# Four late sums in the change-over to the down projection, put at other places of a written order

## The chip, the cores and the metric

The kernel runs on one core of one Trainium2 chip. The metric is the device time of one execution, in microseconds (us), as the median of the runs shown. The core has five engines that work side by side, each through its own list of instructions in order: TensorE (PE in the profile, its weight loads PEld) for matrix products, VectorE (DVE) and ScalarE (ACT) for work on elements, GpSimd (POOL) and SyncE (SP). SP and POOL also issue the DMA transfers here. Engines wait for one another, and for transfers, by semaphores.

## The reference

The kernel computes one layer of a hybrid decoder in float32, for 512 tokens of width 2048. Cut to what matters here, the second half of the layer:

```python
up = h @ w_ffn_in                      # [512, 2048] x [2048, 2 * 5632]
a, b = up[..., :D_FF], up[..., D_FF:]
a = causal_conv3(a) + conv_b
f = (gelu(a) * b) @ w_ffn_out          # [512, 5632] x [5632, 2048]: the down projection
y = x + rmsnorm(f, ffn_post_norm)
```

Ahead of it stand the token mixer (linear attention and differential attention on one input projection, then an output projection) and the norms.

## The kernel before, in words

**Products.** A float32 operand is split into a rounded high half and a remainder. ACT writes the high half (line 138 for weights, line 151 for activations), DVE the remainder (lines 139 and 152), and PE takes three products of halves: lines 1298 to 1300 in the up projection, lines 1400 to 1402 in the down projection. A piece of weights of 128 by 1024 numbers, 512 KB, is called a granule. In the down projection a granule feeds 12 products of 128 by 512.

**Seven products for eight.** Both projections of the channel mixer are cut into 2 by 2 blocks, and seven products with sums of blocks take the place of eight (a Strassen scheme in Winograd's form). A unit of work has seven segments, x0, z0, y0, z1, x1, y1 and y2, of two granules each. The sums of weight blocks are made by DVE and by transfers that add in place, which POOL issues. The sums of the token side, s5, s2, s7 and s3, are made from the output of the up projection's units by `token_sums`: s5 = a21 - a22, s2 = s5 - a11, s7 = a11 - a21, s3 = s2 + a12. Each is one DVE instruction of 128 by 512 elements (line 1373), and a store of 256 KB to DRAM (the tensors `sd0` to `sd4`) follows it, issued by SP in `put`. The four tiles come from a pool of two buffers (`tag="sum", bufs=2`). The last group of units hands its four sums over as functions in the list `late_sums`, in the order s5, s2, s7, s3, to be called later. What they store is read again by the last units of the down projection only.

**The order of the work.** Most of the kernel is ordered by a planner that simulates the engines and places each instruction where it expects it to be ready. The change-over from the last up unit `u` to the first two down units `d0` and `d1` is written out by hand in `change_over` and issued by `run_in_order`, which keeps the written order on PE, ACT, DVE and POOL. It walks through 22 granules: the segments x0 of d0; y1, x1, y2 of u; z0, y0, z1, x1 of d0; x0 of d1; y1 and y2 of d0. At each step it first splits the weights up to three granules ahead (`make`), then issues the granule's products, then, behind a segment's second granule, the reading out of the PSUM banks (`out`, through `into`: ACT at line 1406 for the first write of a place, DVE at line 1408 where it adds), and last the functions that `at` has hung on this segment and granule. Instructions that come after the written block (the rest of d1 first) may still be drawn by the planner into places among the block's last ones.

**A bank that is read and continued.** The segments x0, y0, y1 and y2 of a unit add into one pair of banks. So the first product of y2 into a bank waits until y1's reading of that bank is done.

Of the kernel before, what the change touches and what calls it, by code (L numbers as in the profile page):

```python
# [35 lines left out]
def hybrid_layer(ctx: ExitStack, tc: tile.TileContext, x, attn_pre_norm, w_in, w_alpha_up, b_alpha,  # L36
# [1416 lines left out]
    def at(u, seg, g, *fs):  # L1453
        hooks.setdefault((u, seg, g), []).extend(fs)

    def load_unit(u):
        u.t = [load_t(u.block(0, 0, g), u.a) for g in range(2)]
        u.b22, u.b21 = [], []

    def load_b(u, name, i, j, by=None):  # L1460
        getattr(u, name).extend(load(u.block(i, j, g), u.a, by) for g in range(2))

    def add_t(u, name, g):
        tt(u.t[g], u.t[g], getattr(u, name)[g], ALU.add)
# [13 lines left out]
    def prepare_at(c, n, load_at, split_at):  # L1478
        f, g = prepare_parts(c, n)
        at(*load_at, f)  # L1480
        at(*split_at, g)
# [41 lines left out]
    def change_over(u):  # L1523
        d0, d1 = downs[:2]
        order = [(d0, "x0"), (u, "y1"), (u, "x1"), (u, "y2")]
        order += [(d0, g) for g in ("z0", "y0", "z1", "x1")] + [(d1, "x0"), (d0, "y1"), (d0, "y2")]
        at(d0, "x0", 0, lambda: load_b(d0, "b22", 1, 1))
        at(d0, "x0", 0, late_tiles)
        at(d0, "x0", 1, lambda: (add_t(u, "b21", 0), add_t(u, "b21", 1)))
        at(u, "x1", 1, lambda: load_b(d0, "b21", 1, 0))  # L1530
        at(d0, "z0", 1, lambda: load_unit(d1))
        prepare_at(0, "s2", (d0, "x0", 1), (u, "y2", 0))
        prepare_at(0, "s3", (u, "y1", 1), (d0, "z0", 0))
        prepare_at(0, "a12", (u, "x1", 0), (d0, "z0", 1))
        prepare_at(0, "s7", (u, "x1", 1), (d0, "y0", 1))
        prepare_at(0, "a22", (u, "y2", 0), (d0, "z1", 1))
        for g in range(2):
            at(u, "y2", g, lambda g=g: add_t(d0, "b22", g))
        at(d0, "z1", 0, lambda: add_t(d0, "b21", 0))
        at(d0, "x1", 0, lambda: add_t(d0, "b21", 1))  # L1540
        for where in ((d0, "y0", 0), (d0, "x1", 1), (d1, "x0", 0), (d1, "x0", 1)):
            at(*where, lambda: late_sums.pop(0)())
        return order

    order = change_over(ups[-1])
    u = ups[-1]
    u.b21 = [load(u.block(1, 0, g), u.a) for g in range(2)]
# [217 lines left out]
```

## Time and profile before

| | us |
|---|---|
| median of the runs | 2078.0 |
| runs | 2084.13, 2075.84, 2078.0 |
| the profiled execution, its own time | 2077.34 |
| its span, from first to last instruction | 2075.6 |
| PE busy in the span | 2048.7 |
| DVE busy | 1508.4 |
| ACT busy | 1000.0 |
| POOL busy | 291.9 |

A row of the profile's timeline gives the start in us from the beginning of the span, the duration, the engine, the line of the kernel, the operation and `out<-in`; brackets tell how long the engine had stood idle before and what ended the wait. In the table of waits a row reads: who waited, for whom, the sum in us, how many times, the longest. The chain of waits follows the work that ended last back in time. Rows by stretch of time give, for each engine, the busy us and the number of instructions, and then the granted clock of PE (1.00 is full speed), the share of time in which the transfer engines were busy, and GB/s. A row of a transfer ends in the KB of one and the median us from issue to landing.

### The profile page before, as it was taken

The page shows a single profiled execution, that of the slowest core. Times are in us where ns is not written, and L with a number is a line of the kernel's source. Part 1 is how long each engine was busy: PE and PEld are TensorE (multiplying, and loading weights), DVE is VectorE, ACT ScalarE, POOL GpSimd, SP SyncE. Part 2 cuts the span into 40 slices and gives each one's busy share as a digit, 9 for nine tenths or more (in the row PEclk, how much of TensorE's full clock was granted, in tenths as well). Part 3 has the DMA queues.
Part 4 walks back from the last instruction along what each step waited for, and adds up shares of the span by engine and source line. Part 5 has one row for each costly group of instructions (what it writes and reads, how often), then busy time and mean ns, then how long its engine had stood idle before and what let it go on. Part 6 is the DMA issues. An engine that isn't in the chain of part 4 may idle for free.

```text
span 2075.6 us, 35519 instructions
## 1 busy us (share of the span) xinstructions
PE 2048.7 (99%) x14429; PEld 1896.9 (91%) x14429; DVE 1508.4 (73%) x1793; ACT 1000.0 (48%) x1303; POOL 291.9 (14%) x306
## 2 busy tenths in 40 slices
PE   7999999999999999999999999999999999999998
PEld 6799999999988889899999999999999978888886
DVE  5967777666762255977777777777777888988977
ACT  5544444455552243454554554454455654544433
POOL 0112222222200000011011011111110111111100
PEclk9999999999999999999999999999999999999999
DMA  5488888888883354457667578577667886776663
GB/s 213 121 187 185 192 197 182 196 174 200 193 259 125 94 177 146 124 112 197 149 148 195 142 163 191 131 171 179 141 162 196 214 237 185 188 196 182 165 181 122
DMA packets 281465, 358.61 MB, mean 173 GB/s; under 512 B 14848, under 2 KB 223156, under 8 KB 279380
## 3 DMA queue, kind: packets, MB, share of 16 engines
q1 hardware_dynamic: 192148, 259.85, 37.4%
q0 software_dynamic: 84800, 94.38, 30.1%
q10 hardware_dynamic: 4352, 2.10, 0.4%
q8 instruction: 113, 1.85, 0.4%
q14 instruction: 52, 0.43, 0.1%
HBM read 311.72 MB, written 44.56 MB: 172 GB/s over the span
## 4 chain that ended last, share of the span: by engine, by line
PE 93%; DVE 2%; DMA 2%; issue 1%; ACT 1%; POOL 1%; DVEq 0%; SPq 0%; POOLq 0%; ACTq 0%
PE bank L1298 12%; PE bank L1299 12%; PE bank L1300 12%; PE bank L1400 6%; PE bank L1401 6%; PE bank L1402 6%; PE bank L193 3%; PE bank L192 3%; PE bank L194 3%; PE bank L793 3%; PE bank L795 3%; PE bank L794 3%; PE bank L797 2%; PE bank L798 2%; PE bank L799 2%; PE bank L176 2%
## 5 line engine op out<-in xcount | busy, mean ns | idle before, releaser
L138 ACT ACTIVATE ring<-raw 128x1024 fp32r<-128x1024 f32 x315 | 333.7, 1061 | 499.1 <-PE bank L1299 113.1
L139 DVE TENSOR_TENSOR ring<-raw,ring 128x1024 fp32r<-128x1024 f32 x315 | 383.5, 1223 | 259.3 <-ACT ring L138 256.0
L138 ACT ACTIVATE ring<-rt 128x1024 fp32r<-128x1024 f32 x221 | 234.5, 1061 | 259.3 <-PE bank L1299 154.0
L1299 PE MATMUL bank<-al,ring 128*128 128x256 f32 x1280 | 354.0, 277 | 0.0
L1298 PE MATMUL bank<-ah,ring 128*128 128x256 f32 x1280 | 354.0, 277 | 0.0
L1300 PE MATMUL bank<-ah,ring 128*128 128x256 f32 x1280 | 353.9, 277 | 0.0
L139 DVE TENSOR_TENSOR ring<-rt,ring 128x1024 fp32r<-128x1024 f32 x221 | 270.2, 1223 | 91.2 <-ACT ring L138 90.2
L1298 PEld LDWEIGHTS bank<-ah,ring 128*128 128x128 f32 x1280 | 240.5, 188 | 0.1
L1299 PEld LDWEIGHTS bank<-al,ring 128*128 128x128 f32 x1280 | 240.4, 188 | 0.1
L1300 PEld LDWEIGHTS bank<-ah,ring 128*128 128x128 f32 x1280 | 240.4, 188 | 0.0
L1402 PE MATMUL bank<-ring,al 128*128 128x512 f32 x424 | 165.8, 391 | 0.0
L1401 PE MATMUL bank<-ring,ah 128*128 128x512 f32 x424 | 165.7, 391 | 0.0
L1400 PE MATMUL bank<-ring,ah 128*128 128x512 f32 x424 | 153.2, 392 | 2.2 <-DVE acc L1408 2.2
L193 PE MATMUL bank<-ring,ah 128*128 128x512 f32 x280 | 109.8, 393 | 0.0
L192 PE MATMUL bank<-ring,ah 128*128 128x512 f32 x280 | 109.6, 397 | 0.0
L194 PE MATMUL bank<-ring,al 128*128 128x512 f32 x280 | 109.3, 393 | 0.0
L1246 POOL DMA_DIRECT2D raw<-in_w_ffn_in_dram x40 | 51.2, 1309 | 396.4 <-DVE ring L139 396.4
L1400 PEld LDWEIGHTS bank<-ring,ah 128*128 128x128 f32 x424 | 79.9, 188 | 19.7 <-DVE acc L1408 3.1
L1246 POOL DMA_DIRECT2D rt<-in_w_ffn_in_dram x40 | 50.9, 1279 | 325.9 <-DVE ring L139 303.4
L1402 PEld LDWEIGHTS bank<-ring,al 128*128 128x128 f32 x424 | 79.9, 189 | 16.7
L1401 PEld LDWEIGHTS bank<-ring,ah 128*128 128x128 f32 x424 | 79.9, 188 | 16.4
L797 PE MATMUL bank<-ring,ah 128*128 128x256 f32 x320 | 92.1, 288 | 1.0 <-ACT ah L151 1.0
(378 smaller groups left out, 5661.8 us busy)
## 6 DMA issues: line engine op xcount, KB each, us to landing
raw<-in_w_ffn_in_dram SPq DMA_DIRECT2D x96, 512.0 KB, 4.8
raw<-in_w_in_dram SPq DMA_DIRECT2D x56, 512.0 KB, 4.5
raw<-in_w_ffn_out_dram SPq DMA_DIRECT2D x46, 512.0 KB, 6.0
raw<-in_w_in_dram POOLq DMA_DIRECT2D x40, 512.0 KB, 7.2
rt<-in_w_ffn_in_dram SPq DMA_DIRECT2D x40, 512.0 KB, 6.1
rt<-in_w_ffn_in_dram POOLq DMA_DIRECT2D x40, 512.0 KB, 6.2
raw<-in_w_ffn_in_dram POOLq DMA_DIRECT2D x40, 512.0 KB, 6.9
raw<-in_w_o_dram SPq DMA_DIRECT2D x32, 512.0 KB, 3.9
```

The source lines that it names most:

```text
L138: act(hi, raw, AF.Copy)
L139: tt(lo, raw, hi.bitcast(F32), ALU.subtract)
L192: mm(banks[t], ah[:, t, s, :], w[0][:, k, :], start=st, stop=False)
L193: mm(banks[t], ah[:, t, s, :], w[1][:, k, :], start=False, stop=False)
L194: mm(banks[t], al[:, t, s, :], w[0][:, k, :], start=False, stop=sp)
L797: mm(o, sh[:, n, kk, :], wh[:, k, :], start=st, stop=False, **NOW)
L1298: mm(o, wh, sh[:, :, kk, :], start=start and kk == 0 and n == 0, stop=False, **NOW)
L1299: mm(o, wh, sl[:, :, kk, :], start=False, stop=False, **NOW)
L1300: mm(o, wl, sh[:, :, kk, :], start=False, stop=kk == HK - 1, **NOW)
L1400: mm(b[j], sh[:, o:o + P], w[0][:, q, :], start=start and st == 0, stop=False, **NOW)
L1401: mm(b[j], sh[:, o:o + P], w[1][:, q, :], start=False, stop=False, **NOW)
L1402: mm(b[j], sl[:, o:o + P], w[0][:, q, :], start=False, stop=st == 3, **NOW)
```

## The change

One line of `change_over` names the places at which the four functions of `late_sums` are called. A place is a unit, a segment and a granule of it.

```diff
-        for where in ((d0, "y0", 0), (d0, "x1", 1), (d1, "x0", 0), (d1, "x0", 1)):
+        for where in ((d0, "y0", 0), (d0, "y0", 0), (d0, "x1", 1), (d0, "y1", 1)):
             at(*where, lambda: late_sums.pop(0)())
```

In the order of the 22 granules, counted from 0, the calls stood at 10 (s5), 15 (s2), 16 (s7) and 17 (s3). They now stand at 10 (s5), 10 (s2), 15 (s7) and 19 (s3). The functions, their number and their order are as they were:

```python
def add(n, x, y, op):
    def go():
        t = made[n] = fp.tile([P, 2, 256], F32, name=n, tag="sum", bufs=2)
        tt(t, made.get(x, x) if isinstance(x, str) else x, y, op)
        put(n, t)
    return go
```

## The prediction

> **What bounds the kernel now.** I read the busy shares first, then the waits of PE over the whole span, then the chain of waits around the one place that the change touches, and last the timelines of DVE and SP there.
>
> ```profile
> PE 2048.7 (99%) x14429; PEld 1896.9 (91%) x14429; DVE 1508.4 (73%) x1793; ACT 1000.0 (48%) x1303; POOL 291.9 (14%) x306
> ...
> PE bank L159 <- DVE xt L248: 10.6, 2, 9.6
> PE bank L1400 <- DVE acc L1408: 2.2, 1, 2.2
> PE bank L797 <- ACT ah L151: 1.0, 1, 1.0
> ```
>
> PE is busy for all but 27 us of its 2075.6 us. The longest waits are at the start (line 159). The largest after that is a single one of 2.2 us, of a product of the down projection (line 1400) for a reading of a bank by DVE (line 1408). No other exceeds 1.0 us. So a change to this kernel can win only what such waits cost. The chain of waits says what stands behind the 2.2 us:
>
> ```profile
> 1669.75 0.25 DVE s L1373
> 1670.02 7.93 DMA sd4s<-s
> 1678.31 0.34 issue
> 1678.65 0.37 DVE xlo L139
> ...
> 1679.79 0.69 DVE acc L1408
> 1680.52 0.50 PE bank L1400
> ```
>
> A sum of line 1373 is stored at 1670.02, the store takes 7.93 us, and only when it has landed, at 1677.95, does DVE go on; then follow a weight split, the reading of the bank, and PE's product at 1680.52. The DVE timeline shows which sum is which:
>
> ```profile
> 1652.83 0.69 DVE L1373 TENSOR_TENSOR s<-u 128x512 f32<-128x512 f32 x1
> 1654.95 1.23 DVE L152 TENSOR_TENSOR al<-st,ah 128x1024 fp32r<-128x1024 f32 x1 [1.44 <-ACT ah L151]
> ...
> 1667.57 0.69 DVE L1373 TENSOR_TENSOR s<-s,u 128x512 f32<-128x512 f32 x1
> 1668.17 1.22 DVE L139 TENSOR_TENSOR ring<-raw,ring 128x1024 fp32r<-128x1024 f32 x1
> 1669.31 0.68 DVE L1373 TENSOR_TENSOR s<-u 128x512 f32<-128x512 f32 x1
> 1669.91 1.22 DVE L139 TENSOR_TENSOR ring<-rt,ring 128x1024 fp32r<-128x1024 f32 x1
> 1671.05 1.22 DVE L152 TENSOR_TENSOR al<-st,ah 128x1024 fp32r<-128x1024 f32 x1
> 1673.55 1.23 DVE L139 TENSOR_TENSOR ring<-rt,ring 128x1024 fp32r<-128x1024 f32 x1 [1.29 <-ACT ring L138]
> 1678.04 0.69 DVE L1373 TENSOR_TENSOR s<-s,u 128x512 f32<-128x512 f32 x1 [3.27 <-DMA sd4s<-s]
> 1678.65 1.22 DVE L139 TENSOR_TENSOR xlo<-rt,xhi 128x1024 fp32r<-128x1024 f32 x1
> 1679.79 0.68 DVE L1408 TENSOR_TENSOR acc<-acc,bank 128x512 f32<-128x512 f32 x1
> 1680.39 1.22 DVE L1263 TENSOR_TENSOR rt<-rt,raw 128x1024 f32<-128x1024 f32 x1
> 1681.52 0.68 DVE L1408 TENSOR_TENSOR acc<-acc,bank 128x512 f32<-128x512 f32 x1
> ```
>
> The four rows of line 1373 are s5, s2, s7, s3 in this order. s3 at 1678.04 had waited 3.27 us for the store issued at 1670.02, which is that of s7 (added at 1669.31), not that of s2. So s3 writes into s7's buffer: s2 is still an operand of s3 and holds the other one. Behind s3 in DVE's list stand the last split of y2 (1678.65) and the two readings of d0's y1 (1679.79 and 1681.52), one for each bank, and PE's y2 needs these.
>
> **What the stall costs PE.** It is more than 2.2 us:
>
> ```profile
> 1660.00:1675.00 15.00, 15.00 (x68) 12.42 (x67) 13.49 (x15) 7.34 (x8) 2.37 (x2) 1.00 1.05 289
> 1675.00:1690.00 15.00, 12.78 (x49) 9.74 (x48) 10.31 (x11) 5.65 (x7) 1.17 (x1) 0.89 0.82 261
> 1690.00:1705.00 15.00, 15.00 (x68) 12.43 (x67) 12.30 (x12) 10.77 (x13) 2.36 (x2) 1.00 0.66 172
> ...
> 1682.00:1685.40 3.40, 3.38 (x8) 2.48 (x8) 3.40 (x4) 0.18 (x1) 0.63 (x1) 0.50 0.61 226
> ...
> 1700.00:1800.00 100.00, 100.00 (x443) 82.86 (x442) 87.72 (x92) 49.09 (x49) 12.41 (x11) 1.00 0.75 205
> ```
>
> PE started 49 products in the 15 us around the stall, and 68 in the 15 us before and after. At 100 us / 443 = 0.226 us each the 19 missing ones are 4.3 us. The parts: PE's last start before the gap and its next one are
>
> ```profile
> 1677.70 0.61 PE L1400 MATMUL bank<-ring,ah 128*128 128x512 f32 x2
> 1680.52 0.50 PE L1400 MATMUL bank<-ring,ah 128*128 128x512 f32 x1 [2.21 <-DVE acc L1408]
> ```
>
> two products from 1677.70, so the next was due at 1678.15 and came 2.37 us late. Then the granted clock stood at 0.50 from 1682.00 to 1685.40, where 3.4 us do the work of 1.7. The rest, 0.2 us, is the second bank: its reading ended at 1681.52 + 0.68 = 2.2, and its product came at 1682.25, two tenths behind its turn. 2.37 + 1.7 + 0.2 = 4.3 us.
>
> The half clock is counted with the stall because the trace has full clock before and after it, and keeps full clock across shorter gaps: a stretch in which PE idled for 1.9 us, the wait of 1.0 us of line 797 among it, stays at 1.00.
>
> ```profile
> 590.00:600.00 10.00, 8.09 (x70) 7.68 (x69) 9.45 (x13) 6.28 (x11) 0.00 (x0) 1.00 0.45 146
> ```
>
> [...]
>
> **The change, part by part.** Nothing is added or removed: four sums of 0.69 us (each takes 0.60 us of DVE's turn: 1667.57 to 1668.17) and four stores of 256 KB. Each is followed in turn.
>
> *s2, from granule 15 to 10.* It now follows s5, at 1653.43 in before's times. Its operand s5 is DVE's own result just made. DVE was idle there for 1.44 us until 1654.95, for ACT; 0.60 us fit. Cost nothing; if that cover were gone, 0.6 us of DVE, still behind splits made three granules (8 us) ahead. Its store is issued at about 1654.1, where SP had nothing to issue until 1656.21:
>
> ```profile
> 1653.54 0.32 SPq L48 DMA_DIRECT2D sd4s<-s  x1
> 1656.21 0.32 SPq L48 DMA_DIRECT2D st<-sd1a  x1
> ...
> 1668.28 0.34 SPq L48 DMA_DIRECT2D sd4s<-s  x1
> ...
> 1678.76 0.32 SPq L48 DMA_DIRECT2D sd4s<-s  x1
> ```
>
> *s7, from 16 to 15.* It takes the place s2 had, 1667.57, and waits for s5's store. That left at 1653.54 and took 5.2 us (row below), so it has been landed for 8.8 us. Its own store leaves at 1668.28, where s2's did. Cost nothing. DVE has one sum fewer at 1669.31, so the split of y2's first granule comes 0.6 us sooner.
>
> *s3, from 17 to 19.* This is the step that counts. In the list it moves behind the last split of y2 and behind both readings of y1. So that split can go as soon as ACT has the high half:
>
> ```profile
> 1670.95 1.05 ACT L138 ACTIVATE xhi<-rt 128x1024 fp32r<-128x1024 f32 x1
> ```
>
> that is at 1672.0 in place of 1678.65, in the 1.29 us for which DVE now idles ahead of 1673.55. (The split at 1673.55 is that of a granule of d1 which the planner has drawn forward.) y1 ends on PE at 1674.98, by its last product:
>
> ```profile
> 1674.75 0.39 PE L1402 MATMUL bank<-ring,al 128*128 128x512 f32 x1
> ```
>
> Its first bank is complete six products (1.36 us) sooner, so DVE reads it at about 1674.0, or at 1674.7 if d1's split (1673.55 to 1674.7) stays ahead. PE now follows y1 with 14 products drawn forward from d1 (1674.98 to 1678.15, 14 x 0.226 = 3.2 us) before y2. If the planner keeps them, the bank is read 2.8 us in time. If y2 follows y1 directly, PE waits 1674.7 + 0.68 - 1674.98 = 0.4 us at worst, under the 1.0 us that left the clock alone. So the stall goes, with bounds of 3.9 and 4.3 us on the gain; I take 4.3.
>
> What is late next is s3 itself. It comes up on DVE behind the second reading, at about 1675.3 (y1's last product ends at 1675.14) + 0.68 = 1676.0, and waits for s7's store, now issued at 1668.28:
>
> ```profile
> raw<-in_w_ffn_out_dram POOLq DMA_DIRECT2D x1, 512.0 KB, 11.0
> sd4s<-s SPq DMA_DIRECT2D x1, 256.0 KB, 5.2
> ...
> sd4s<-s SPq DMA_DIRECT2D x1, 256.0 KB, 7.9
> ```
>
> With 5.2 us it has landed at 1673.5, with 7.9 us at 1676.2: a wait of 0 to 0.2 us. Behind s3 in DVE's list are the weight sums of line 1263 and the split of d1's second granule of z0, 0.6 + 1.13 + 1.13 = 2.9 us with s3. PE needs that split after y2 (24 products) and z0's first granule (12): 1674.98 + 36 x 0.226 = 1683.1. So s3 may start as late as 1680.2, and the store may take up to 11.9 us. On SP, s3's store stood blocked until 1678.76 with other transfers behind it in the queue, and PE shows no wait for a transfer later; it now goes sooner.
>
> **Sum.** 2077.34 (the profiled execution; 0.66 below the median of 2078.0, inside the runs' 2075.84 to 2084.13) - 4.3 = 2073.0 us. PE is the bound on both sides of the place (no wait of PE in the span is later than this one), so the gain reaches the end.
>
> **The rivals.**
>
> *Part of the stall comes back through the planner (0.09).* The written block fixes only its own order. Behind it the planner places by simulated times, and these change: it drew a granule of d1 ahead of y2 in before, and may place line 1263 or a split ahead of y1's readings. One such piece is 1.13 us; behind 1674.7 it makes PE wait 0.4 + 1.13 = 1.5 us, between the 1.0 that kept the clock and the 2.2 that lost it. The price is 1.5 to 3.2 us: 2074.5 to 2076.2. For it speaks that 1680.39 stands between the two readings; against it, that every later unit has the same join without a wait.
>
> *The clock would have dropped anyway (0.05).* If the half clock belonged to some earlier load and not to the gap, only 2.37 + 0.2 = 2.6 us go: 2074.7. [...] Against it: the clock is full in every row shown before the gap.
>
> *The change does not do what it says (0.04).* If s3's wait came from something other than s7's store and moved along with it, nothing goes: 2077.3. The 1677.95 against 1678.04 speaks against this.
>
> *Slower: s7's store lands late and s3 blocks DVE (0.04).* The place is DVE's list behind y1's second reading. From 11.9 us on, each further us is PE idle at z0's second granule; from 2.2 us of idling the half clock comes to it. The kernel gets slower from an idle of 2.4 us, a store of 14.3 us. At 16 us: 4.1 + 1.7 = 5.8 us, 2073.0 + 5.8 = 2078.8. Transfers are dense there (share 1.05), but the slowest row here took 11.0 us at double the size.
>
> *More is won (0.02).* The other waits that could go with it by a new order are 1.0 us and less: 2071.
>
> **How the numbers follow.** The forecast has 0.76: 2073.0, by itself 2071.5 (the lowest run less 4.3) to 2075. The range 2071.0 to 2078.0 takes in the planner's case, the clock's and no effect, and leaves out the slower case and runs disturbed by more. About 0.5% (10.4 us) is what a measurement of this kernel can tell from no change. No case reaches it: the gain is bounded by the 4.3 us, and the slower case would need a store of over 20 us. I leave 0.02 on either side for an order of the planner that I have not seen, 0.96 within.
>
> **What would show it.** In the changed profile line 1373 has no wait for a store at sd4's last sum, or one under 0.5 us; the wait of line 1400 for line 1408 is gone; a window of 15 us there holds 67 or 68 products, and the clock stays at 1.00 there. s2's row follows s5's within 0.7 us. The prediction is wrong if PE shows a new wait over 1 us behind y1, if s3 waits over 4 us, or if PE's waits are gone and the end does not come 4 us sooner.

## The result, and the profile after

The changed kernel takes 2073.2 us in the median of 20 runs (2070.57 to 2077.91), the kernel before 2077.16 us in the median of 20 (2073.94 to 2084.72). The ratio is 0.9981, with a 95% interval of 0.9973 to 0.9988. The medians lie 4.0 us apart, and the interval allows 2.5 to 5.6. The forecast was 2073.0, 4.3 us less, and no difference over 0.5%.

The waits of PE over the span of the changed kernel (who waited, for whom, us in total, times, longest):

```profile
PE bank L159 <- DVE xt L248: 11.6, 3, 9.7
PE bank L1300 <- DVE ring L139: 2.3, 4, 0.8
PE bank L797 <- ACT ah L151: 1.3, 1, 1.3
```

The wait of line 1400 for line 1408, 2.2 us before, is gone. Busy time by stretch (span, then PE, PEld, DVE, ACT, POOL with their counts, granted clock, share of transfers, GB/s):

```profile
1660.00:1675.00 15.00, 15.00 (x68) 12.42 (x67) 15.00 (x16) 9.06 (x10) 2.37 (x2) 1.00 1.06 265
1675.00:1690.00 15.00, 15.00 (x68) 12.43 (x67) 13.00 (x13) 8.06 (x10) 1.17 (x1) 1.00 1.04 350
```

Each stretch of 15 us holds 68 products, where the one around the stall had held 49, and the clock stays at 1.00. The DVE timeline of the changed kernel shows how the four sums of line 1373 now lie. The down projection starts 4.9 us later in this execution than in the one shown of before (1625.1 and 1620.2, below), so 4.9 is to be taken off when the two are laid side by side:

```profile
1657.75 0.69 DVE L1373 TENSOR_TENSOR s<-u 128x512 f32<-128x512 f32 x1
1658.47 0.69 DVE L1373 TENSOR_TENSOR s<-s,u 128x512 f32<-128x512 f32 x1
1659.87 1.22 DVE L152 TENSOR_TENSOR al<-st,ah 128x1024 fp32r<-128x1024 f32 x1 [0.71 <-ACT ah L151]
...
1672.49 0.69 DVE L1373 TENSOR_TENSOR s<-u 128x512 f32<-128x512 f32 x1
...
1676.95 1.23 DVE L139 TENSOR_TENSOR xlo<-rt,xhi 128x1024 fp32r<-128x1024 f32 x1 [0.20 <-ACT xhi L138]
1678.47 1.23 DVE L139 TENSOR_TENSOR ring<-rt,ring 128x1024 fp32r<-128x1024 f32 x1 [0.29 <-ACT ring L138]
1679.61 0.68 DVE L1408 TENSOR_TENSOR acc<-acc,bank 128x512 f32<-128x512 f32 x1
1680.21 1.22 DVE L1263 TENSOR_TENSOR rt<-rt,raw 128x1024 f32<-128x1024 f32 x1
1681.35 0.68 DVE L1408 TENSOR_TENSOR acc<-acc,bank 128x512 f32<-128x512 f32 x1
1681.94 0.68 DVE L1373 TENSOR_TENSOR s<-s,u 128x512 f32<-128x512 f32 x1
```

s3, the last row, has no bracket: it waits for nothing. The last split of y2 (1676.95) and the readings of y1 (1679.61, 1681.35) stand ahead of it. s7's store, in SP's timeline and then as a transfer (KB, us to landing):

```profile
1673.20 0.34 SPq L48 DMA_DIRECT2D sd4s<-s  x1
```

```profile
sd4s<-s SPq DMA_DIRECT2D x1, 256.0 KB, 8.0
```

The store took as long as before (8.0 us, 7.9 then) and landed at 1681.2, 0.7 us ahead of s3.

**The spans do not show the gain, the stage does.** The changed kernel's profiled execution took 2077.91 us (span 2076.2), that of before 2077.34 (span 2075.6). So I compare the stage, from the first to the last product of line 1400 that reads weights from `ring`. The row has x count, min/median/max ns, then the start of the first and of the last; the kernel before stands first, then the changed one:

```profile
L1400 PE MATMUL bank<-ring,ah x424: 388/390/793, 1620.2 to 2021.4; 128*128 128x512 f32 x142
```

```profile
L1400 PE MATMUL bank<-ring,ah x424: 389/389/397, 1625.1 to 2021.9; 128*128 128x512 f32 x142
```

The stage took 2021.4 - 1620.2 = 401.2 us before and 396.8 us after: 4.4 us less. What the changed kernel lost in its profiled execution lies ahead of this stage, where the two kernels have the same instructions in the same order on every engine.

### The profile page after: what moved, and what is told of

It is laid out like the page before. It is cut to its first block, busy times and chain, and to the rows that moved or that the text cites. A ratio compares the mean times of both kernels' runs of the same rounds, so it can differ in the third digit from the quotient of the medians.

```text
span 2076.2 us, 35516 instructions
## 1 busy us (share of the span) xinstructions
PE 2048.1 (99%) x14429; PEld 1896.1 (91%) x14429; DVE 1506.8 (73%) x1793; ACT 999.1 (48%) x1303; POOL 291.3 (14%) x306
## 4 chain that ended last, share of the span: by engine, by line
PE 62%; issue 28%; DMA 3%; POOL 3%; DVE 2%; ACT 1%; POOLq 0%; DVEq 0%; SPq 0%; ACTq 0%
PE bank L1400 6%; PE bank L1401 6%; PE bank L1402 6%; PE bank L192 3%; PE bank L193 3%; PE bank L194 3%; PE bank L793 3%; PE bank L795 3%; PE bank L794 3%; PE bank L1300 3%; PE bank L1299 3%; PE bank L1298 3%; PE bank L797 2%; PE bank L799 2%; PE bank L798 2%
```

## The experiments

The theory: DVE works through its list in order; s3 stands there waiting for the store of s7 (3.27 us in the trace of before), whose buffer it takes; behind it stands work that PE needs at once. Each experiment below is timed against the kernel before on the same chip, and its profile gives the length of the stage as above.

| kernel | places of s5, s2, s7, s3 | median us | before us | ratio (95%) | stage us |
|---|---|---|---|---|---|
| before | 10, 15, 16, 17 | | | | 401.2 |
| changed | 10, 10, 15, 19 | 2073.2 | 2077.16 | 0.9981 (0.9973 to 0.9988) | 396.8 |
| e1, s2 alone | 10, 10, 16, 17 | 2079.6 | 2076.7 | 1.0015 (1.0006 to 1.0024) | 404.3 |
| e2, s3 alone | 10, 15, 16, 19 | 2073.31 | 2076.7 | 0.9983 (0.9974 to 0.9992) | 396.8 |
| e3, s7 alone | 10, 15, 15, 17 | 2078.97 | 2076.7 | 1.0009 (1.0001 to 1.0018) | 403.1 |
| e4, own buffer | 10, 15, 16, 17 | 2072.59 | 2076.7 | 0.9981 (0.9972 to 0.999) | 396.8 |
| e5, both late | 10, 10, 19, 19 | 2071.91 | 2076.42 | 0.9979 (0.997 to 0.9988) | 396.8 |
| e6, between | 10, 15, 16, 18 | 2074.51 | 2076.42 | 0.9988 (0.9978 to 0.9999) | 398.2 |

**e2: s3 alone.**

```diff
-        for where in ((d0, "y0", 0), (d0, "x1", 1), (d1, "x0", 0), (d1, "x0", 1)):
+        for where in ((d0, "y0", 0), (d0, "x1", 1), (d1, "x0", 0), (d0, "y1", 1)):
```

> Only s3 is moved, from granule 17 to 19, behind the readings of y1; s2 and s7 stay at 15 and 16. Theory: this is the whole of the change's gain, s3's wait of 0 to 1.9 us falls behind the readings of y1 and is covered; 4.3 us gained, about 2073 us, a window of 15 us at the place holds 67 or 68 products and the clock stays full. Rival (the gain needs the wider spacing of the stores too): part of the stall stays, 2075 to 2077 us.

The whole gain is there: the same stage of 396.8 us. In its DVE timeline s3 still waits for a store, but behind the readings of y1 and not ahead of them:

```profile
1677.38 1.28 DVE L1408 TENSOR_TENSOR acc<-acc,bank 128x512 f32<-128x512 f32 x2
...
1680.38 0.69 DVE L1373 TENSOR_TENSOR s<-s,u 128x512 f32<-128x512 f32 x1 [1.73 <-DMA sd4s<-s]
```

The wait of 1.73 us costs nothing there. So the move of s3 is the change; the wider spacing of the other sums adds nothing that can be measured.

**e4: no move, but s3 in a buffer of its own.**

```diff
-                t = made[n] = fp.tile([P, 2, 256], F32, name=n, tag="sum", bufs=2)
+                t = made[n] = fp.tile([P, 2, 256], F32, name=n, tag="p1" if n == "s3" and gi == NG - 1 else "sum", bufs=2)
```

> All four sums stay at the places of the kernel before, but the last group's s3 is written into a buffer of another pool that has been free for some time, so it waits for no store. Theory: the wait of s3 goes and the stall with it, although nothing moved; 4.3 us gained, about 2073 us, no wait for a store ahead of s3. Rival (the stall comes from DVE being full in this stretch, which the new places thin out): the stall stays, 2077 us.

The four sums stand where they stood before, and the stage is 396.8 us. The DVE timeline has s3 without a wait, 1.74 us behind s7:

```profile
1668.34 0.68 DVE L1373 TENSOR_TENSOR s<-u 128x512 f32<-128x512 f32 x1
1670.08 0.68 DVE L1373 TENSOR_TENSOR s<-s,u 128x512 f32<-128x512 f32 x1
```

So it was the shared buffer, and not the number of DVE instructions in the stretch.

**e1: s2 alone.**

```diff
-        for where in ((d0, "y0", 0), (d0, "x1", 1), (d1, "x0", 0), (d1, "x0", 1)):
+        for where in ((d0, "y0", 0), (d0, "y0", 0), (d1, "x0", 0), (d1, "x0", 1)):
```

> Only s2 is moved, from granule 15 to 10, beside s5; s7 and s3 stay at 16 and 17. Theory (the stall is s3 waiting on DVE for the store of s7): the wait stays, since s7 still stands one granule ahead of s3. The store would leave about 0.6 us sooner, at 1669.4 in the times of the kernel before, and land 5.2 to 7.9 us later. The planner has put the split of d1's first granule behind s3 in this kernel's list, so PE may stop right behind y1, for 2.6 to 5.3 us, and lose the clock with it: 4.3 to 7.0 us lost against 4.3 in the kernel before, so 2077 to 2080 us. Rival (moving any one sum out of the crowded stretch is enough): the stall goes, 2073 us.

Slower than before, by 2.9 us in the medians and 3.1 us in the stage. SP, DVE and PE in its timelines:

```profile
1652.64 1.05 SPq L48 DMA_DIRECT2D sd4s<-s  x2
1668.51 0.34 SPq L48 DMA_DIRECT2D sd4s<-s  x1
```

```profile
1676.16 0.69 DVE L1373 TENSOR_TENSOR s<-s,u 128x512 f32<-128x512 f32 x1 [5.24 <-DMA sd4s<-s]
1676.77 1.22 DVE L139 TENSOR_TENSOR xlo<-rt,xhi 128x1024 fp32r<-128x1024 f32 x1
1677.91 1.22 DVE L139 TENSOR_TENSOR ring<-rt,ring 128x1024 fp32r<-128x1024 f32 x1
```

```profile
1679.18 0.79 PE L1401 MATMUL bank<-ring,ah 128*128 128x512 f32 x1 [4.50 <-DVE ring L139]
```

The wait for the store stays. s2's store left beside s5's, 15 us before s7's (1668.51), and s3 waits until 1676.16 all the same. So it is s7's store that s3 waits for.

The wait costs more here. In the kernel before, the planner, which places d1's first split freely, had put it ahead of s3; here it stands behind s3 (1677.91). PE had its products of d1 next and stopped for their split. The median lies in the range that I had given, but the loss against the changed kernel's stage, 7.5 us, is above its 4.3 to 7.0: the half clock lasted 6.8 us (row in the last section). The same order of DVE is in e3.

**e3: s7 alone.**

```diff
-        for where in ((d0, "y0", 0), (d0, "x1", 1), (d1, "x0", 0), (d1, "x0", 1)):
+        for where in ((d0, "y0", 0), (d0, "x1", 1), (d0, "x1", 1), (d1, "x0", 1)):
```

> Only s7 is moved, from granule 16 to 15, right behind s2; s3 stays at 17. Its store leaves about 1.1 us sooner than before, at 1668.9, and lands 5.2 to 7.9 us later. Theory: s3 still waits ahead of the readings of y1, and here the planner has put the split of d1's first granule behind s3, so PE stops behind y1 for 2.1 to 4.8 us and with the half clock loses 3.8 to 6.5 us: 2076.5 to 2079 us. Rival (two granules between s7 and s3 are enough): 2073 us.

The stage takes 403.1 us, 1.9 more than before: PE idles 4.4 us and has the half clock for 3.4 us behind it. Its rows of DVE and of PE, and then the stretch of the half clock:

```profile
1677.73 0.69 DVE L1373 TENSOR_TENSOR s<-s,u 128x512 f32<-128x512 f32 x1 [4.58 <-DMA sd4s<-s]
```

```profile
1680.75 0.50 PE L1401 MATMUL bank<-ring,ah 128*128 128x512 f32 x1 [4.40 <-DVE ring L139]
```

```profile
1681.30:1684.70 3.40, 3.40 (x10) 2.60 (x9) 3.40 (x4) 0.00 (x0) 0.00 (x0) 0.51 0.95 374
```

Two granules between s7 and s3 (5.4 us) are too few for a store of 7.9 us, as expected.

**e6: s3 behind the split, ahead of the readings.**

```diff
-        for where in ((d0, "y0", 0), (d0, "x1", 1), (d1, "x0", 0), (d1, "x0", 1)):
+        for where in ((d0, "y0", 0), (d0, "x1", 1), (d1, "x0", 0), (d0, "y1", 0)):
```

> s3 at granule 18, so behind the last split of y2 but still ahead of the readings of y1; s7 at 16 as in the kernel before. Theory: the split is not what PE lacked, the reading of the bank is. s3 goes at 1678.0 if the store takes 7.9 us again, the reading ends at about 1679.3, and PE, which wants it at 1678.15 behind 14 products of d1, idles about 1.2 us: 1.2 to 1.5 us lost with a full clock (a gain of about 3 us, 2074.4 us), or 3.1 us with the half clock (2076 us); the gap lies between 1.0 us, which kept the clock, and 2.2 us, which lost it. With a store of 5.2 us nothing is lost. Rival (the late split at 1678.65 was the cause): the whole 4.3 us are gained, no idling, 2073 us.

The rows of DVE, of PE, and of the stretch:

```profile
1677.93 0.69 DVE L1373 TENSOR_TENSOR s<-s,u 128x512 f32<-128x512 f32 x1 [3.29 <-DMA sd4s<-s]
1678.54 1.28 DVE L1408 TENSOR_TENSOR acc<-acc,bank 128x512 f32<-128x512 f32 x2
```

```profile
1679.27 0.50 PE L1400 MATMUL bank<-ring,ah 128*128 128x512 f32 x1 [1.10 <-DVE acc L1408]
```

```profile
1675.00:1690.00 15.00, 13.89 (x61) 11.14 (x61) 12.00 (x12) 8.31 (x10) 1.17 (x1) 1.00 0.78 257
```

s3 waits as long as before (3.29 us), but the split is now ahead of it, and PE idles 1.10 us for the reading. The clock stays at 1.00. The stage is 1.4 us longer than the changed kernel's and 3.0 shorter than that of before. So with the split out of the way the late reading alone still stops PE. The split's move took one instruction (1.13 us) out of the gap, and behind the gap of 1.10 us the clock stayed full: 3.0 of the 4.4 us. The last 1.4 us are got by putting s3 behind the readings.

**e5: s7 and s3 both behind the readings, nothing between them in the order of granules.**

```diff
-        for where in ((d0, "y0", 0), (d0, "x1", 1), (d1, "x0", 0), (d1, "x0", 1)):
+        for where in ((d0, "y0", 0), (d0, "y0", 0), (d0, "y1", 1), (d0, "y1", 1)):
```

> s5 and s2 at granule 10, s7 and s3 both at 19, s3 behind s7 with no granule between them, both behind the readings of y1. Theory: what counts is not the distance between the two that share a buffer but whether PE soon needs something behind s3 in DVE's list. s7's store leaves at about 1676.7 in the times of the kernel before and lands at 1681.9 to 1684.6. The planner has put two splits and a weight sum between s7 and s3, so DVE idles up to 3.4 us at s3, and the next split is ready at the latest at about 1686.4, against PE's need at about 1685.9: 0 to 0.5 us of idling, 0 to 1 us lost, 2073 to 2074 us. Rival (the distance of the sharers is what counts): the stall is as before or worse, 2077 us and more.

```profile
1675.68 0.68 DVE L1373 TENSOR_TENSOR s<-u 128x512 f32<-128x512 f32 x1
...
1679.93 0.69 DVE L1373 TENSOR_TENSOR s<-s,u 128x512 f32<-128x512 f32 x1
```

Neither row waits for a store, and the stage is the same 396.8 us. So no granule is needed between the two that share a buffer, once both stand behind the readings. In time they are not close: the planner has put 3.6 us of other work between them, and no wait was left that would have had to be covered. That such a wait is covered is shown by e2 alone. My working was off in one term: the store of s7, issued behind the first row, had landed when s3, which takes its buffer, began: in under 3.6 us (1676.36 to 1679.93), where I had given it 5.2 to 7.9. That it had landed is read from s3's start without a wait; the profile lists no landing of this store.

**Two repeats.** Both kernels ran once more for a second profile.

> The kernel before as it is, for a second profile. In the profile of the changed kernel the down projection's first product came 4.9 us later than in that of before, although the lists of instructions are the same up to there; there ACT waited for weight loads near 1006, 1403 and 1481 us. If that is chance of an execution, the first product of line 1400 will lie anywhere from 1620 to 1626 us in a second profile, and s3's wait and the half clock behind it will be there as before.

> The changed kernel as it is, for a second profile. If the late loads of its first profile were chance, the first product of line 1400 will not lie at 1625 us again as a rule, and PE will have no wait at the place of the change.

The row of line 1400 in the kernel before, and then in the changed one:

```profile
L1400 PE MATMUL bank<-ring,ah x424: 388/389/628, 1619.9 to 2020.9; 128*128 128x512 f32 x142
```

```profile
L1400 PE MATMUL bank<-ring,ah x424: 389/389/397, 1619.3 to 2016.1; 128*128 128x512 f32 x142
```

The stage takes 401.0 and 396.8 us, against 401.2 and 396.8 in the first pair. In the kernel before, s3 waits again (3.41 us), PE idles 2.4 us behind it, and the granted clock over the 20 us from 1670 is 0.91, as it is in the first profile of before. The rows of PE's wait and of the stretch:

```profile
PE bank L1400 <- DVE acc L1408: 2.4, 1, 2.4
```

```profile
1670.00:1690.00 20.00, 17.65 (x72) 14.09 (x71) 13.88 (x14) 8.80 (x12) 1.17 (x1) 0.91 0.87 278
```

In the changed one PE has no wait between 1650 and 1690, and the clock over the same 20 us is 1.00. The start at 1625.1 does not come back; that of the kernel before lies at 1619.9, a tenth outside the range that I had given. Over all ten profiles the stage starts between 1618.9 and 1625.1.

## Why the prediction was right

**The cost of the stall** was the sum, 2.37 idle, 1.7 of half clock and 0.2: 4.3 us. The stage is 4.4 us shorter, the medians of the runs 4.0 us apart, the ratio allows 2.5 to 5.6. So the size rests on the stage: 4.4 us in the first pair of profiles, 4.2 in the second. The same way of counting, the idle time and half of the PE work that ran at half clock, gives 6.1 us for e3 (4.40 + 1.7), 7.4 for e1 (4.50 + 5.8 / 2) and 1.1 for e6; measured against 396.8 us are 6.3, 7.5 and 1.4.

The forecast of 2073.0 stands against 2073.2. That it is so near is luck in part. The 4.3 us were taken off one execution of 2077.34, which turned out to lie 0.2 us from the median of 20; off the median then known, 2078.0, they give 2073.7. I had also put what a measurement can tell from no change at about 0.5%; with 20 runs of each kernel, a change of 0.2% was clear.

**Whose store s3 waits for.** The chain had it as s7's. e1 shows that it is not s2's, whose store had left 15 us earlier while s3 waited all the same. e4 shows that the shared buffer makes the wait: with another buffer for s3 and nothing moved, the wait and the stall are gone.

**The length of the wait does not set the price.** The sums of the earlier groups share two buffers as well. In the kernel before, DVE waits for their stores nine times between 875 and 1620 us, for up to 3.2 us. Two of these rows (us in total, times, longest):

```profile
DVE s L1373 <- DMA sd3s<-s: 5.7, 2, 3.2
DVE s L1373 <- DMA sd1s<-s: 5.5, 2, 3.1
```

PE has no wait in that time. So waits about as long as the 3.27 us of s3 cost nothing there; the 4.4 us came from what stood behind s3, as the prediction had it.

**s2 and s7 cost nothing.** s2 lies 0.72 us behind s5 and took its time out of DVE's wait for ACT, which fell from 1.44 to 0.71 us. s7 waits for nothing.

**s3's new place.** In the times of before, the last split was to come at 1672.0 and the first reading at 1674.7 behind d1's split; they came at 1676.95 - 4.9 = 1672.05 and 1679.61 - 4.9 = 1674.7. s3 was to come at 1676.0 and came at 1677.0, as the planner left the weight sum of line 1263 between the two readings, where it had been; I had put it behind s3. The store took 8.0 us, a tenth over my range. Neither touched PE.

**The rivals.** That the clock would have dropped anyway falls: it dropped at this place in the four profiles with a gap of 2.2 us or more there (before, its repeat, e1, e3: 0.83 to 0.91 over the 20 us from 1670) and in none of the other six (1.00). That the planner gives part of the stall back did not happen in the changed kernel, but e1 and e3 show that it can: there its order made the same wait dearer than before. A late store was nearer than I had put it in one respect, 0.7 us ahead of s3; but e2 shows a wait of 1.73 us there at no cost, so the cover behind the readings is real. I had worked it out as 4 us, and that size was not tested. The slower case was priced a little wrong: with a gain of 4.3 us and 1.7 us of half clock, it begins at an idle of 2.6 us and not 2.4. No run came near it.

**What was badly chosen** is one of my own signs: that the end of the changed profile must come 4 us sooner. It came 0.6 us later in the first pair of profiles and 4.8 us sooner in the second (2075.2 and 2070.4). One execution's span differs by more than this change from causes ahead of the place; the stage's length does not.

## What to carry to other kernels

A wait of a few us on an engine that is not the bound is priced by what stands behind it in that engine's list: here waits of up to 3.2 us cost PE nothing, and one of 3.27 us cost it 4.4. Look there for what the bounding engine needs next, and move the waiting instruction behind it, or give it a buffer that is free. When tiles share a pool, work out from the trace which store actually frees the buffer; here it was that of the third sum, not of the second. Compare a change of a few us on the stage that it touches, between two products that both profiles have, not on the spans.

## What I had not expected of the hardware

**At this place the half clock came in pieces of 3.4 us, behind gaps of 2.2 us and more.** Gaps of PE of 1.0, 1.1 (e6) and 1.6 us (the wait of line 797 in e5) kept the clock:

```profile
PE bank L797 <- ACT ah L151: 1.6, 1, 1.6
```

```profile
590.00:600.00 10.00, 8.45 (x75) 8.23 (x74) 8.96 (x13) 6.28 (x10) 0.00 (x0) 1.00 0.54 170
```

The gap of 2.2 us in the first profile of before brought 3.4 us at half clock, and so did 4.4 us in e3. Behind the 2.4 us of the second profile of before I estimate as much: a clock of 0.91 over 20 us is 1.8 us lost, and 3.4 us at half clock lose 1.7. The gap of 4.5 us in e1 brought 6.8 us:

```profile
1678.20:1685.00 6.80, 5.82 (x14) 4.57 (x15) 5.59 (x7) 1.06 (x1) 0.00 (x0) 0.50 0.57 211
```

In e1 the half clock began 1.0 us before PE's next product (1679.18), in the kernel before 1.5 us after it. At the start of the span PE of before waited 9.6 us, and no half clock followed: the clock from 10 to 20 us is 1.00. So the length of the gap alone does not tell. What sets the start and the length of the pieces is not shown, and no gap between 1.6 and 2.2 us was tried.

**A store of 256 KB took from under 3.6 us, by s3's start in e5, to 8.0 us** in this one stretch of the kernel. It is not the share of the transfer engines that tells these two apart. The rows of the changed kernel from the issue of s7's store to its landing, and of e5 from the issue to s3's start:

```profile
1673.20:1681.20 8.00, 8.00 (x37) 6.64 (x36) 7.42 (x7) 5.21 (x6) 0.00 (x0) 1.00 1.03 320
1676.39:1679.93 3.54, 3.54 (x17) 2.96 (x16) 3.39 (x3) 1.27 (x2) 0.75 (x1) 1.00 0.98 360
```

The engines were busy throughout in both (1.03 and 0.98). What differs is how much they moved while the store was on its way: 2.6 MB at 320 GB/s in 8.0 us, and at most 1.3 MB at 360 GB/s in 3.54 us. Whether the transfers that were already under way made the long one late was not tested.

**Loads of the up projection were late in some executions.** The waits of ACT for weights between 875 us and the change-over, in the first profile of the changed kernel and then in its second:

```profile
ACT ring L138 <- DMA raw<-in_w_ffn_in_dram: 69.1, 22, 5.1
```

```profile
ACT ring L138 <- DMA raw<-in_w_ffn_in_dram: 49.1, 19, 4.1
```

A stretch of the up projection, in the same two profiles:

```profile
1400.00:1500.00 100.00, 98.35 (x858) 97.54 (x857) 71.99 (x71) 48.40 (x55) 12.79 (x10) 1.00 0.68 162
```

```profile
1400.00:1500.00 100.00, 100.00 (x885) 100.00 (x884) 76.30 (x76) 49.06 (x57) 14.04 (x11) 1.00 0.68 163
```

27 products fewer in 100 us, at 100 / 885 = 0.113 us each, are 3.1 us of the 5.8 by which the stage began later than in the second profile (1625.1 and 1619.3). That the late loads are what held PE there is read from these rows and was not tested; what makes the loads late in one execution and not in another stays open.
